# Convolution activations of a hybrid decoder layer mixed head by head and kept in DRAM

## The chip, the cores and the metric

The kernel runs on one core of one Trainium2 chip. The core has a matrix engine (TensorE, PE in the profile, with PEld for its weight loads), a vector engine (VectorE, DVE), a scalar engine (ScalarE, ACT), GpSimd (POOL) and SyncE (SP), which only issues transfers. Sixteen DMA engines move data between DRAM and the on-chip memory; here they are fed from two queues, SP's and POOL's. The metric is device time in microseconds of one execution, as the median of several runs. A profiled execution has a time of its own, which is given beside its span.

## The reference

One decoder layer on 528 tokens (16 learned meta tokens and a sequence of 512) of width 2048, in fp32:

```python
n = _rmsnorm(h, g_mix[l])
p = n @ w_in[l]
q, k, v, gb, gc, u = jnp.split(p, ...)            # six groups of 1024 columns
q = _rmsnorm(q.reshape(b, L, 8, 128), g_q[l]);  k = _rmsnorm(k.reshape(...), g_k[l])
o_attn = _stick_breaking_attention(q, k, v).reshape(b, L, 1024)
o_conv = gb * _causal_dwconv(gc * u, conv_w[l])   # 3 taps, one filter per channel
o = concat([_rmsnorm(o_attn, g_attn_out[l]), _rmsnorm(o_conv, g_conv_out[l])])
h = h + o @ w_out[l]
n2 = _rmsnorm(h, g_ffn[l])
h = h + (silu(n2 @ w_gate[l]) * (n2 @ w_up[l])) @ w_down[l]
```

The attention weights of a query t on a key s < t are beta[t,s] times the product of (1 - beta[t,j]) over the keys between them, computed in log space with a reverse cumulative sum. The meta positions are dropped from the output.

## The kernel before

All activations are held transposed: 128 channels on the partitions (a "k tile", 16 of them), tokens along the free dimension. To keep fp32 precision, each operand of a product is split into a high part (a cast to fp32r, on ACT) and a low part (the difference, on DVE), and each product is three matmuls: high x high, high x low, low x high. The helper split does this for activations, split_quad for weights.

The layer goes through these stages.

1. Start. SP loads the first weight pieces and the 16 tiles xt of x; ACT and DVE scale them by g_mix and split them into nh and nl (n_parts), which stay on chip. The products for k and q of head 0 run while this goes on (product_steps). Then read_qk evicts them.
2. Heads 0 to 7 (head). Each head's products for k, q and v run on PE over all 16 k tiles; the attention of the head (attend) is put between the matmuls of the next products: after(n, work) emits work n k tiles later, when tick has counted them. The masks of attend are made on POOL (causal). At the end of a head its output o is scaled and split into a tile st_o (a pool with two places) and stored to oa_dram on POOL's queue.
3. Convolution. The products for the first channel tile (pc0, pu0, pb0) and for pb1 run in the plain way. The other channel tiles go in pairs (conv_pair, gate_pair) by a scheme with seven block products in place of eight: pair_product. It takes two weight columns over two halves of the k tiles (four 512 KB weight blocks, "quads" 11, 12, 22, 21) and two halves of the tokens. Three weight operands are sums of quads (t1, t2, t3), and seven activation operands stand against the seven weights, in the order of conv_acts: a raw block of nh/nl, three mixed blocks (mixed), a last mixed block (last_block), and two more raw blocks.
4. The output projection, then the feed-forward in 44 pairs and the down projection by the same scheme. The change does not touch these.

The mixed blocks are differences of quarter blocks of x: with a0, a1 the two token halves of k tile k and b0, b1 those of k tile k + 8, they are d = b1 - a1, e = -d - a0, f = -e - b0, and for the last block a0 - a1. In the kernel before, mix_x (L706) is called for the eight k one after the other at L727, behind the work of the last head. For each k it loads the two rows of x again on POOL's queue, scales them on ACT, forms the four blocks on DVE, and splits three of them into the tiles mixed. The fourth is kept in late and is split at L737 over columns of nh and nl, which must not be read any more by the product pb1. pair_product for the first pair then starts with the product of the raw block 0 (x), goes on with the three mixed ones (z, x, z), the last block (x), the raw block 5 (y) and the raw block 6 (x).

What sets the order of the work: the program is written as one stream, and a scheduler orders each engine's instructions by its own estimate and by priorities; prepare marks weight splits as high priority, and tc.keep_in_program_order pins single instructions. Each engine and each queue runs its instructions in their order, and an instruction that waits holds up those behind it. Weights: next_w hands out split pieces and has two more prepared ahead; there are three places for split pieces, so a split waits until PE has finished the piece three before it. A loaded piece's place is loaded anew (load_wide, load_quad, load_next, on SP's queue) as soon as its split is done. For pairs in the "swapped" order (FIRST_ORDER, L223), the 21 quad is split first and used for the y product at the head of the pair; in the kernel before, that is the first feed-forward pair (i == CONV) alone.

Of the kernel before, what the change touches and what calls it, by code (L numbers as in the profile page):

```python
# [9 lines left out]
F32 = mybir.dt.float32  # L10
# [5 lines left out]
P = 128  # L16
# [17 lines left out]
def hybrid_layer(ctx: ExitStack, tc: tile.TileContext, xT, w_in, w_out, w_gu, w_down, vecs, out):  # L34
# [141 lines left out]
    def load_wide(g, i):  # L176

        if i < len(groups_w[g]):
            wide[g, i] = w_place(sw_in, 8, i % 4)
            nc.sync.dma_start(wide[g, i], groups_w[g][i])  # L180
        else:
            load_quad((0, CONV)[g], QUADS[i % 4])

    def load_next(i, q):

# [39 lines left out]
    def prepare():  # L225
        kind, i, s = pieces[len(split_w)]
        with tc.high_priority():
            if kind == "first":
                at = len(split_w)
                split_quad(raws[at], s - i, at % 6)  # L230
                if at % 2 and s % 8 == 0:
                    load_wide(0, s // 8 + 1)
                return
            if kind == "wide":
                split_quad(wide[i, s], 8)
                load_wide(i, s + 4)
                return
            n, swapped = pairs[i][0], i == CONV
            if swapped:
                s = FIRST_ORDER[s]  # L240
            b = {q: quads[i, q] for q in ("11", "12", "21", "22") if (i, q) in quads}
            if s == 0:
                split_quad(b["11"], n)
                add_quads(i, "t1", b["11"], b["12"])
                load_next(i, "11")
            elif s == 1:
                split_quad(sums["t1"], n)
                sums["t2"] = sums["t1"]
                ve.tensor_tensor(sums["t2"], sums["t2"], b["22"], ALU.add)
                if not swapped:  # L250
                    add_t3(i, b)
            elif s == 2:
                split_quad(sums["t2"], n)
                if swapped:
                    add_t3(i, b)
            elif s == 3:
                split_quad(b["22"], n)
                load_next(i, "22")
            elif s == 4:
                split_quad(sums["t3"], n)  # L260
            elif s == 5:
                split_quad(b["21"], n)
                if not swapped:
                    add_last(i, b)
            else:
                if swapped:
                    add_last(i, b)
                split_quad(sums["t2"], n)
                if i + 1 == SIX:
                    load_quad(SIX + 1, QUADS[1])  # L270

    def next_w():
        ahead = max(min(n_first, used[0] + 6), used[0] + 1 + S_AHEAD)
        while len(split_w) < min(len(pieces), ahead):
            prepare()
        used[0] += 1
        return split_w[used[0] - 1]
# [134 lines left out]
        for k in range(max(a, 1), b):  # L412
            load_x(k)
    for i in range(2):
        load_wide(0, i)
    for a, b in FIRST:
        for k in range(a, b):
            split_x(k)
# [13 lines left out]
    kns = [apool.tile([P, 640], F32, name=f"kn{i}") for i in range(1)]  # L432
    for t in kns:
        gp.memset(t[:, L:640], 0.0)
    accp.tile([P, 48], F32, name="pad_acc")
    acc_c = accp.tile([P, SEQ], F32, name="acc_c")
    acc_a = accp.tile([P, SEQ], F32, name="acc_a")

    stpool = open_pool("stpool")
    oa_dram = [dram.tile([P, 2, SEQ], F32R, name=f"oa_dram{h}") for h in range(HEADS)]  # L440

    def qk_norm(read, dst, parts_of, name):

# [25 lines left out]
    def head(h):  # L469

        if h:
            pk = pp.tile([P, 2, 512], F32, tag="pp", name=f"pk{h}")
            product([(pk[:, 0, :H], 0, H), (pk[:, 1, :H], H, L)], n_hl)
        read = read_qk(halves(pk, H), g_k, L) if h else read_k0
        kn = kns[0]
        kh = apool.tile([P, 384], F32R, tag="kh", name=f"kh{h}")
        kl = apool.tile([P, 384], F32R, tag="kl", name=f"kl{h}")
        after(8 if h else 19, qk_norm(read, kn[:, :L], (kh, kl, 384), f"k{h}"))

        if h:  # L480
            pq = pp.tile([P, 2, 512], F32, tag="pp", name=f"pq{h}")
            product([(pq[:, 0, :], META, L)], n_hl)
        read = read_qk(pq[:, 0, :], gq_s, SEQ) if h else read_q0
        qn = apool.tile([P, SEQ], F32, tag="qn", name=f"qn{h}")
        qh = apool.tile([P, SEQ], F32R, tag="qh", name=f"qh{h}")
        ql = apool.tile([P, SEQ], F32R, tag="ql", name=f"ql{h}")
        after(9 if h else 22, qk_norm(read, qn, (qh, ql, SEQ), f"q{h}"))

        pv = pp.tile([P, 2, 512], F32, tag="pp", name=f"pv{h}")
        product([(pv[:, 0, :H], 0, H), (pv[:, 1, :H], H, L)], n_hl)  # L490
        vt = t512(L, "e", 2)
        with tc.high_priority(0 if h else 1 << 20):
            ve.tensor_tensor(two(vt[:, :L]), halves(pv, H), two(r), ALU.mult)
        after(6 if h else 15, lambda: attend(h, kn, kh, kl, qn, qh, ql, vt))

    def attend(h, kn, kh, kl, qn, qh, ql, vt):
# [98 lines left out]
        def mix(ws):  # L595
# [7 lines left out]
            pe.matmul(o[:, Q0[3] :], v32[:, :P], lw[:, 1184:1328], start=False, stop=False)  # L603
            pe.matmul(o[:, Q0[4] :], v32[:16, P:], lw[:16, 1328:1344], start=False, stop=True)
            g = g_att[:, h : h + 1]
            st = stpool.tile([P, 2, SEQ], F32R, tag="st_o", bufs=2, name=f"st_o{h}")
            sc.activation(st[:, 0], o, AF.Copy, scale=g)
            ve.scalar_tensor_tensor(st[:, 1], o, g, st[:, 0].bitcast(F32), ALU.mult, ALU.subtract)
            square_sum(acc_a, o, h == 0)
# [21 lines left out]

    N = T2 + 2
    C0 = META - 2
# [11 lines left out]
    def gated(p, j, y, gb, s):  # L647
# [2 lines left out]
        square_sum(acc_c, p, j == 0, s, ve)  # L650
        sc.activation(p, p, AF.Copy, scale=g_cnv[:, j : j + 1])

    pc = cu_product("pc0")
    cu0 = t512(L, "e", 2)[:, : SEQ + 2]
    ve.tensor_tensor(cu0[:, :T2], pc[:, 0, :T2], r2[:, C0 : C0 + T2], ALU.mult)
# [9 lines left out]
    ve.tensor_tensor(gb0, pb[:, 0, :], r[:, META:], ALU.mult)  # L665
    assert not waiting
    apool.release()
    stpool.release()
    ocpool = open_pool("ocpool")

# [7 lines left out]
    const.release()  # L678

    mixp = open_pool("mixp")  # L680
    mixed = [mixp.tile([P, 8, 2, N], F32R, name=f"mixed{i}") for i in (1, 2, 3)]
    ctmp = open_pool("ctmp", side="right")

    def raw_block(kh, th, a=0, n=N):
# [1 line left out]
        return lambda part, k: n_parts[k + 8 * kh][part][:, at : at + n]  # L686

    def mixed_block(t, a=0, n=N):
        return lambda part, k: t[:, k, part, a : a + n]

    def last_block(a=0, n=N):
        return lambda part, k: n_parts[k][part][:, C0 + N + a : C0 + N + a + n]
# [8 lines left out]
        ]  # L701

    CN = SEQ + 2
    late = ctmp.tile([P, 8, N], F32, tag="late", name="late")

    def mix_x(k):  # L706

        x = []
        for i in range(2):
            if k % 2:  # L710
                x.append(ctmp.tile([P, 3 * N], F32, tag="sides", name=f"x{k}_{i}") if i else ctmp.tile([P, CN], F32, tag="b0", name=f"x{k}_{i}"))
                x[i] = x[i][:, :CN]
            else:
                x.append(ctmp.tile([P, CN], F32, tag="cu", bufs=2, name=f"x{k}_{i}"))
            gp.dma_start(x[i], xT[k + 8 * i][:, C0:])
            sc.activation(x[i], x[i], AF.Copy, scale=g_mix[:, k + 8 * i : k + 8 * i + 1])
        (a0, a1), (b0, b1) = ([t[:, i * T2 : i * T2 + N] for i in range(2)] for t in x)
        d, e = (oc_slot(1 + m, F32, f"mix{k}_{m}")[:, :N] for m in (k % 2, 2))
        ve.tensor_tensor(d, b1, a1, ALU.subtract)
        split(mixed[0][:, k, 0], mixed[0][:, k, 1], d)  # L720
        ve.scalar_tensor_tensor(e, d, -1.0, a0, ALU.mult, ALU.subtract)
        split(mixed[1][:, k, 0], mixed[1][:, k, 1], e)
        ve.scalar_tensor_tensor(d, e, -1.0, b0, ALU.mult, ALU.subtract)
        split(mixed[2][:, k, 0], mixed[2][:, k, 1], d)
        ve.tensor_tensor(late[:, k], a0, a1, ALU.subtract)

    for k in range(8):  # L727
        mix_x(k)
    gb1 = oc_slot(7, F32, "gb1")
    pb = pp.tile([P, 2, 512], F32, tag="pp", name="pb1")  # L730
    product([(pb[:, 0, :], META, L)], n_hl)
# [3 lines left out]
    xyz = open_pool("xyz", 2, space=PSUM)  # L735
    sm = open_pool("sm2", 1, space=PSUM)
    for k in range(8):  # L737
        split(*(n_parts[k][part][:, C0 + N : C0 + 2 * N] for part in range(2)), late[:, k])
    sides_c = ctmp.tile([P, 3 * N], F32, tag="sides", name="sides_c").rearrange("p (a b) -> p a b", a=3)

    def wide_product(ps, acts):
        hi, lo = next_w()
# [27 lines left out]
    def pair_product(acts, cols, out2, side, fourth=None):  # L770
# [30 lines left out]
    def conv_pair(j):  # L801
        u = ctmp.tile([P, CN], F32, tag="cu", bufs=2, name=f"cu{j}")
        y, last = pair_product(conv_acts(), N, [u[:, t * T2 : t * T2 + N] for t in range(2)], [sides_c[:, t] for t in range(3)])
        ve.tensor_tensor(u, u, r2[:, C0:], ALU.mult)
        c = sides_c[:, 0, :T2]
        ve.tensor_tensor(c, y[:, :T2], c, ALU.add)
        ve.tensor_tensor(u[:, :T2], u[:, :T2], c, ALU.mult)
        x = last()
        ve.tensor_tensor(u[:, T2:], x, u[:, T2:], ALU.mult)
        ocf[j] = ctmp.tile([P, 8 * N], F32, tag="late", name="y6")[:, :SEQ] if j == 6 else oc_slot(min(j, 6), F32, f"y{j}")  # L810
        conv3(ocf[j], u, j)

    def gate_pair(j):
# [10 lines left out]
        gated(ocf[j - 1], j - 1, ocf[j - 1], b0, b0)  # L824

    def scale_a():
        w = ctmp.tile([P, 8 * N], F32, tag="late", name="work_a")
        w = [w[:, i * SEQ : (i + 1) * SEQ] for i in range(3)]
# [377 lines left out]
```

## Time and profile before

| | |
|---|---|
| median of 3 runs | 2065.96 us (2065.57 to 2066.32) |
| the profiled execution | 2066.83 us, its span 2065.1 us |
| mean granted clock of TensorE | 0.993 |
| DMA | 339.35 MB, mean 164 GB/s |
| POOL's queue | 77616 packets, 124.33 MB |

A row of waits names the engine and the tile that it was about to write, then what it waited for, then the time in total, the number of waits and the longest. A row of a timeline gives the start and the duration in microseconds, the engine and line, the operation, the tiles written and read, shapes and types, and in brackets the idle time of the engine before it. A row of stages gives the stretch, its length, the busy time of PE, PEld, DVE, ACT and POOL with the number of instructions, the granted clock, the busy share of the DMA engines and the rate. Matmul rows overlap: the distance between the starts of two is their pace. In a group, a tile's number is left out, so pb is pb0 and pb1.

### The profile page before, as it was taken

To read this page: it belongs to the slowest core of one execution; us is meant where nothing else is said; L and a number is where in the kernel's file an instruction comes from. 1 tells how busy PE (TensorE), PEld (TensorE's weight loads), DVE (VectorE), ACT (ScalarE), POOL (GpSimd) and SP (SyncE) were. 2 spreads that over 40 slices of the span, in tenths; PEclk is the share of its full clock that TensorE was granted. 3 is DMA by queue.
4 is the path that set the end of the run, shared out by engine and by line. 5 is a ranking of instruction groups with operands and counts; after the bars stand their busy time and mean duration, and the time that the engine had idled before them with its cause. 6 is when DMAs were issued, how large, how long until landed. Compare 5 with 4: busy or idle time off the path is not lost.

```text
span 2065.1 us, 39541 instructions
## 1 busy us (share of the span) xinstructions
PE 2034.2 (99%) x16134; PEld 1968.8 (95%) x16134; DVE 1744.4 (84%) x2243; ACT 1071.1 (52%) x1551; POOL 347.0 (17%) x501
## 2 busy tenths in 40 slices
PE   9999999889999999999999999999999999999999
PEld 8999999789998888999999999999999999999999
DVE  6877777788888778999898898898888888888888
ACT  6666556544444444555455555555555544444443
POOL 0111111200003442111111111011011243121111
PEclk9999999989999999999999999999999999999999
DMA  6222222433345555546545555465555899798764
GB/s 213 76 92 83 93 93 82 140 96 103 103 161 192 168 171 191 164 139 194 169 139 174 159 154 169 149 173 159 147 175 158 255 335 348 191 297 209 218 148 94
DMA packets 145254, 339.35 MB, mean 164 GB/s; under 512 B 12768, under 2 KB 60640, under 8 KB 145072
## 3 DMA queue, kind: packets, MB, share of 16 engines
q1 hardware_dynamic: 67456, 212.50, 32.1%
q0 software_dynamic: 77616, 124.33, 22.9%
q8 instruction: 126, 2.06, 0.4%
q14 instruction: 56, 0.46, 0.1%
HBM read 267.31 MB, written 69.47 MB: 163 GB/s over the span
## 4 chain that ended last, share of the span: by engine, by line
PE 91%; DVE 3%; DMA 3%; ACT 1%; issue 1%; SPq 0%; POOL 0%; DVEq 0%; ACTq 0%; POOLq 0%
PE x L766 13%; PE x L768 13%; PE x L767 13%; PE z L767 6%; PE z L766 6%; PE z L768 6%; PE y L767 3%; PE y L766 3%; PE y L768 3%; PE pv L302 2%; PE pv L303 2%; PE pv L304 2%; PE pq L303 1%; PE pq L304 1%; PE pq L302 1%; PE pk L302 1%
## 5 line engine op out<-in xcount | busy, mean ns | idle before, releaser
L202 ACT CAST sw_split<-sw_in 128x1024 fp32r<-128x1024 f32 (+2 forms) x668 | 661.9, 992 | 708.8 <-PE z L767 190.8
L203 DVE TENSOR_TENSOR sw_split<-sw_in,sw_split 128x1024 fp32r<-128x1024 f32 (+2 forms) x668 | 771.6, 1156 | 165.2 <-ACT sw_split L202 156.8
L766 PE MATMUL x<-f,sw_split 128*128 128x256 f32 x1408 | 387.6, 275 | 0.1
L768 PE MATMUL x<-f,sw_split 128*128 128x256 f32 x1408 | 387.4, 275 | 0.1
L767 PE MATMUL x<-f,sw_split 128*128 128x256 f32 x1408 | 387.3, 275 | 0.0
L766 PEld LDWEIGHTS x<-f,sw_split 128*128 128x128 f32 x1408 | 264.3, 188 | 0.4 <-ACT sides L790 0.3
L768 PEld LDWEIGHTS x<-f,sw_split 128*128 128x128 f32 x1408 | 264.3, 188 | 0.3 <-DVE sw_split L203 0.3
L767 PEld LDWEIGHTS x<-f,sw_split 128*128 128x128 f32 x1408 | 264.3, 188 | 0.1
L1021 POOL DMA_DIRECT2D fd<-s x147 | 103.8, 915 | 711.5 <-DVE s L316 694.8
L209 DVE TENSOR_TENSOR sw_in<-sw_in 128x1024 f32<-128x1024 f32 (+1 forms) x164 | 187.9, 1146 | 10.4 <-DMA sw_in<-w_gu 3.2
L767 PE MATMUL z<-f,sw_split 128*128 128x256 f32 x704 | 193.7, 275 | 1.4 <-DVE f L316 1.4
L766 PE MATMUL z<-f,sw_split 128*128 128x256 f32 x704 | 193.7, 275 | 1.0 <-ACT sides L788 1.0
L768 PE MATMUL z<-f,sw_split 128*128 128x256 f32 x704 | 193.6, 275 | 0.0
L768 PE MATMUL x<-ring,sw_split 128*128 128x256 f32 x608 | 167.3, 275 | 0.5 <-DVE sw_split L203 0.5
L766 PE MATMUL x<-ring,sw_split 128*128 128x256 f32 x608 | 167.2, 275 | 0.0
L767 PE MATMUL x<-ring,sw_split 128*128 128x256 f32 x608 | 167.2, 275 | 0.0
L767 PEld LDWEIGHTS z<-f,sw_split 128*128 128x128 f32 x704 | 132.1, 188 | 1.6 <-DVE f L316 1.6
L766 PEld LDWEIGHTS z<-f,sw_split 128*128 128x128 f32 x704 | 132.1, 188 | 1.2 <-ACT sides L788 1.2
L768 PEld LDWEIGHTS z<-f,sw_split 128*128 128x128 f32 x704 | 132.1, 188 | 0.0
L768 PEld LDWEIGHTS x<-ring,sw_split 128*128 128x128 f32 x608 | 114.1, 188 | 0.7 <-DVE sw_split L203 0.7
L766 PEld LDWEIGHTS x<-ring,sw_split 128*128 128x128 f32 x608 | 114.1, 188 | 0.0
L767 PEld LDWEIGHTS x<-ring,sw_split 128*128 128x128 f32 x608 | 114.1, 188 | 0.0
(609 smaller groups left out, 5486.2 us busy)
## 6 DMA issues: line engine op xcount, KB each, us to landing
sw_in<-w_gu SPq DMA_DIRECT2D x176, 512.0 KB, 4.0
sw_in<-w_in SPq DMA_DIRECT2D x92, 512.0 KB, 3.3
fd<-s POOLq DMA_DIRECT2D x147, 256.0 KB, 5.3
sw_in<-w_down SPq DMA_DIRECT2D x96, 384.0 KB, 4.3
ring<-fd POOLq DMA_DIRECT2D x42, 768.0 KB, 16.7
sw_in<-w_out SPq DMA_DIRECT2D x32, 512.0 KB, 3.5
out_T<-d POOLq DMA_DIRECT2D x54, 256.0 KB, 5.0
sw_in<-w_down SPq DMA_DIRECT2D x16, 512.0 KB, 7.5
```

The source lines that it names most:

```text
L202: sc.copy(hi, src)
L203: ve.tensor_tensor(lo, src, hi.bitcast(F32), ALU.subtract)
L209: return ve.tensor_tensor(sums[name], a, b, ALU.add)
L302: pe.matmul(ps, wh, ah[:, a:b], start=k + i == 0, stop=False)
L303: pe.matmul(ps, wh, al[:, a:b], start=False, stop=False)
L304: pe.matmul(ps, wl, ah[:, a:b], start=False, stop=k + i == last)
L766: pe.matmul(p, hi[:, kk], ah, start=start and j == k == 0, stop=False, skip_group_check=skip)
L767: pe.matmul(p, hi[:, kk], al, start=False, stop=False, skip_group_check=skip)
L768: pe.matmul(p, lo[:, kk], ah, start=False, stop=k == n - 1, skip_group_check=skip)
L1021: gp.dma_start(fd[c][s][:, :, k], t[:, :, i])
```

## The change

The mixed blocks are no longer made behind the last head. Head h from 1 to 7 makes k tile h - 1, and the eighth is made beside pc0. Each k tile is loaded as four pieces of 128x258 (load_mix, on POOL's queue), scaled by two ACT instructions of 516 columns, mixed in place by four DVE instructions of 258, split two blocks at a time into a place of the pool of st_o (stage), and stored as four pieces of 128x516 to DRAM tensors mix_dram, again on POOL's queue. Behind the last head, six loads on POOL's queue bring the three mixed blocks into tiles mixed (two halves each), and sixteen loads bring the last block into the columns of nh and nl. late and its splits are gone.

The first convolution pair takes the swapped order as well: its y product, on a raw block, comes first, and its 21 quad is split first. Two small parts stand beside this: the first two wide weight loads are pinned to program order, and next_w prepares one piece less ahead at the one call where the first pieces run out. Tiles that stood for the first use of a tag in apool are declared ahead, so that places come out the same.

```diff
@@ load_wide / prepare / next_w
-            nc.sync.dma_start(wide[g, i], groups_w[g][i])
-        else:
-            load_quad((0, CONV)[g], QUADS[i % 4])
+            return nc.sync.dma_start(wide[g, i], groups_w[g][i])
+        load_quad((0, CONV)[g], QUADS[i % 4])
...
-            n, swapped = pairs[i][0], i == CONV
+            n, swapped = pairs[i][0], i in (0, CONV)
...
-        ahead = max(min(n_first, used[0] + 6), used[0] + 1 + S_AHEAD)
+        ahead = max(min(n_first, used[0] + 6), used[0] + 1 + S_AHEAD - (used[0] == n_first))
...
-        load_wide(0, i)
+        tc.keep_in_program_order(load_wide(0, i))
@@ new, ahead of the heads
+    mix_dram = [dram.tile([P, 8, 2, N], F32R, name=f"mix_dram{i}") for i in range(4)]
+    xpool2 = open_pool("xpool2")
...
+    def stage(name):
+        return stpool.tile([P, 4 * N], F32R, tag="st_o", bufs=2, name=name)
+
+    def load_mix(k):
+        x = xpool2.tile([P, 4, N], F32, tag="x", name=f"x_mix{k}")
+        for m in range(4):
+            at = C0 + m % 2 * T2
+            gp.dma_start(x[:, m], xT[k + m // 2 * 8][:, at : at + N])
+        return x
+
+    def mix_x(k, x):
+        for i in range(2):
+            sc.activation(x[:, 2 * i : 2 * i + 2], x[:, 2 * i : 2 * i + 2], AF.Copy, scale=g_mix[:, k + 8 * i : k + 8 * i + 1])
+        a0, a1, b0, b1 = (x[:, m] for m in range(4))
+        ve.tensor_tensor(b1, b1, a1, ALU.subtract)
+        ve.tensor_tensor(a1, a0, a1, ALU.subtract)
+        ve.scalar_tensor_tensor(a0, b1, -1.0, a0, ALU.mult, ALU.subtract)
+        ve.scalar_tensor_tensor(b0, a0, -1.0, b0, ALU.mult, ALU.subtract)
+        for m, blocks in ((2, (2, 0)), (0, (1, 3))):
+            st = stage(f"st_x{k}_{m}").rearrange("p (a b n) -> p a b n", a=2, b=2)
+            split(st[:, :, 0], st[:, :, 1], x[:, m : m + 2])
+            for i, block in enumerate(blocks):
+                gp.dma_start(mix_dram[block][:, k], st[:, i])
@@ head
+            x = load_mix(h - 1)
             pq = pp.tile([P, 2, 512], F32, tag="pp", name=f"pq{h}")
...
+        if h:
+            after(5, lambda: mix_x(h - 1, x))
@@ attend
-            st = stpool.tile([P, 2, SEQ], F32R, tag="st_o", bufs=2, name=f"st_o{h}")
+            st = stage(f"st_o{h}")[:, : 2 * SEQ].rearrange("p (a b) -> p a b", a=2)
@@ convolution
+    x = load_mix(7)
+    after(3, lambda: mix_x(7, x))
     pc = cu_product("pc0")
...
-    mixed = [mixp.tile([P, 8, 2, N], F32R, name=f"mixed{i}") for i in (1, 2, 3)]
+    mixed = [[mixp.tile([P, 4, 2, N], F32R, name=f"mixed{i}_{m}") for m in range(2)] for i in (1, 2, 3)]
+    for i, t in enumerate(mixed):
+        for m in range(2):
+            gp.dma_start(t[m], mix_dram[i][:, 4 * m : 4 * m + 4])
...
-    late = ctmp.tile([P, 8, N], F32, tag="late", name="late")
-    def mix_x(k):
...
-    for k in range(8):
-        mix_x(k)
...
     for k in range(8):
-        split(*(n_parts[k][part][:, C0 + N : C0 + 2 * N] for part in range(2)), late[:, k])
+        for part in range(2):
+            gp.dma_start(n_parts[k][part][:, C0 + N : C0 + 2 * N], mix_dram[3][:, k, part])
...
-        first = i == CONV
+        first = i in (0, CONV)
```

More of the change, by code (lines that the diff above doesn't have):

```diff
@@ L434, in hybrid_layer @@
         gp.memset(t[:, L:640], 0.0)
+    for tag, n in (("kh", 384), ("kl", 384), ("sh", L), ("sl", L), ("qn", SEQ), ("qh", SEQ), ("ql", SEQ), ("bh", 288), ("bl", 288)):
+        apool.tile([P, n], F32 if tag == "qn" else F32R, tag=tag, name=f"first_{tag}")
     accp.tile([P, 48], F32, name="pad_acc")
@@ L439, in hybrid_layer @@
     stpool = open_pool("stpool")
+    N = T2 + 2
+    C0 = META - 2
+    mix_dram = [dram.tile([P, 8, 2, N], F32R, name=f"mix_dram{i}") for i in range(4)]
+    xpool2 = open_pool("xpool2")
     oa_dram = [dram.tile([P, 2, SEQ], F32R, name=f"oa_dram{h}") for h in range(HEADS)]
+    def stage(name):
[19 more added lines that the diff above has]
+                gp.dma_start(mix_dram[block][:, k], st[:, i])
     def qk_norm(read, dst, parts_of, name):
@@ L630, in token_scale @@
         rsqrt(dst, v, SEQ, y, t, eng)
-    N = T2 + 2
-    C0 = META - 2
     def cu_product(name):
@@ L667, in hybrid_layer @@
     apool.release()
+    xpool2.release()
     stpool.release()
@@ L688, in mixed_block @@
     def mixed_block(t, a=0, n=N):
-        return lambda part, k: t[:, k, part, a : a + n]
+        return lambda part, k: t[k // 4][:, k % 4, part, a : a + n]
     def last_block(a=0, n=N):
@@ L703, in hybrid_layer @@
     CN = SEQ + 2
-    late = ctmp.tile([P, 8, N], F32, tag="late", name="late")
-    def mix_x(k):
[L708 to L725, printed above, removed]
-    for k in range(8):
-        mix_x(k)
     gb1 = oc_slot(7, F32, "gb1")
@@ L737, in hybrid_layer @@
     for k in range(8):
-        split(*(n_parts[k][part][:, C0 + N : C0 + 2 * N] for part in range(2)), late[:, k])
-    sides_c = ctmp.tile([P, 3 * N], F32, tag="sides", name="sides_c").rearrange("p (a b) -> p a b", a=3)
+        for part in range(2):
+            gp.dma_start(n_parts[k][part][:, C0 + N : C0 + 2 * N], mix_dram[3][:, k, part])
+    sides_c = ctmp.tile([P, 3, N], F32, name="sides_c")
     def wide_product(ps, acts):
@@ L809, in conv_pair @@
         ve.tensor_tensor(u[:, T2:], x, u[:, T2:], ALU.mult)
-        ocf[j] = ctmp.tile([P, 8 * N], F32, tag="late", name="y6")[:, :SEQ] if j == 6 else oc_slot(min(j, 6), F32, f"y{j}")
+        ocf[j] = ctmp.tile([P, SEQ], F32, tag="work0", name="y6") if j == 6 else oc_slot(min(j, 6), F32, f"y{j}")
         conv3(ocf[j], u, j)
@@ L826, in scale_a @@
     def scale_a():
-        w = ctmp.tile([P, 8 * N], F32, tag="late", name="work_a")
-        w = [w[:, i * SEQ : (i + 1) * SEQ] for i in range(3)]
+        w = [ctmp.tile([P, SEQ], F32, tag=f"work{i}", name=f"work_a{i}") for i in range(3)]
         token_scale(acc_a, acc_a, 1024, "a", (oc_slot(6, F32R, "acc_hi"), oc_slot(7, F32R, "acc_lo"), *w))
```

## The prediction

> **What bounds the kernel now.** I read the page's busy times and chain first, then the waits of TensorE (PE), then the stages around the longest wait, then PE's instructions there.
>
> ```profile
> PE 2034.2 (99%) x16134; PEld 1968.8 (95%) x16134; DVE 1744.4 (84%) x2243; ACT 1071.1 (52%) x1551; POOL 347.0 (17%) x501
> PE 91%; DVE 3%; DMA 3%; ACT 1%; issue 1%; SPq 0%; POOL 0%; DVEq 0%; ACTq 0%; POOLq 0%
> ```
>
> PE sets the end: a microsecond in which it stands still, or runs at half clock, is a microsecond of the kernel. Its longest waits:
>
> ```profile
> PE z L766 <- ACT mixed L315: 10.2, 3, 5.1
> PE z L766 <- DVE gb L732: 5.6, 1, 5.6
> PE pv L302 <- ACT tmp L397: 2.3, 1, 2.3
> ```
>
> The first two lie at one place, the first convolution pair, where the mixed blocks are made while PE waits for them. The stages there (PE, PEld, DVE, ACT, POOL busy; granted clock; DMA share; GB/s):
>
> ```profile
> 100.00:380.00 280.00, 280.00 (x1911) 261.82 (x1910) 207.84 (x342) 168.56 (x277) 39.30 (x103) 1.00 0.27 88
> ...
> 396.00:400.00 4.00, 3.11 (x25) 2.89 (x23) 4.00 (x9) 2.45 (x5) 1.16 (x3) 1.00 0.67 192
> 400.00:404.00 4.00, 0.00 (x0) 0.00 (x0) 3.25 (x10) 2.93 (x8) 1.08 (x2) 0.97 0.30 81
> 404.00:412.00 8.00, 4.67 (x15) 3.58 (x15) 7.28 (x20) 6.15 (x14) 2.69 (x5) 0.50 0.49 138
> 412.00:420.00 8.00, 2.32 (x6) 1.50 (x6) 6.93 (x19) 5.58 (x14) 1.07 (x2) 0.50 0.62 189
> 420.00:424.00 4.00, 1.26 (x3) 0.79 (x3) 2.64 (x8) 2.78 (x6) 0.00 (x0) 0.50 0.00 0
> ...
> 428.00:432.00 4.00, 4.00 (x35) 4.00 (x35) 1.22 (x1) 1.45 (x3) 0.00 (x0) 1.00 0.00 0
> ```
>
> In the heads (100 to 380) PE has no gap. From 399 to 428 it is nearly empty, at clock 0.50, while VectorE (DVE) is the busiest. PE's own rows give the size:
>
> ```profile
> 395.78 0.39 PE L625 MATMUL ss_a<-acc_hi,ones_r 128*128 128x512 f32 x1
> 396.01 0.28 PE L766 MATMUL x<-nh,sw_split 128*128 128x258 f32 x1
> ...
> 428.93 0.28 PE L766 MATMUL z<-mixed,sw_split 128*128 128x258 f32 x1
> ...
> 431.79 0.28 PE L766 MATMUL x<-nh,sw_split 128*128 128x258 f32 x1
> ```
>
> One product of 24 matmuls takes 431.79 - 428.93 = 2.86 us unhindered. The pair's first product starts at 396.01, its fifth at 431.79; unhindered that would be 396.01 + 4 x 2.86 = 407.45. The place costs **24.3 us**, half clock included.
>
> **The change, part by part.**
>
> *Taken from the pair.* The 8 calls of mix_x and the 8 late splits leave this place, and with them their waits. The same seven products remain, so the gain is at most 24.3. Putting the y product first leaves the sum of products alone; it moves the first use of a mixed block from 396.01 + 2.86 = 398.9 to 396.01 + 2 x 2.86 = 401.7. Its weights are the "21" quad, the last of the four to be loaded:
>
> ```profile
> 378.36 1.22 DVE L203 TENSOR_TENSOR sw_split<-sw_in,sw_split 128x1024 fp32r<-128x1024 f32 x1
> 384.65 1.05 ACT L202 CAST sw_split<-sw_in 128x1024 fp32r<-128x1024 f32 x1 [1.34 <-PE pb L303]
> ```
>
> The first row is the split of the last wide piece; the quad's load takes that piece's place from 379.6 on and has 5 us until its own split, which takes the turn of the second row. So y can start at 396, and nothing is added.
>
> *Put in its place: loads on POOL's queue.* In the built program the queue holds five 0.13 MB loads into nh/nl, the six mixed loads (128x2064 f32, 1.06 MB each), then eleven more small ones. The fifth waits until PE has read nh2 in pb1: pb1 is 48 matmuls ending at 395.78, at 0.23 each it starts at 384.6, so at 386.7; the mixed loads queue behind that. Behind them POOL has nothing until the row at 608. What a load of this kind takes (two-microsecond stages, the issue, the landing of single ones):
>
> ```profile
> 608.14 2.13 POOL L843 DMA_DIRECT2D oa<-oa_dram  x4 [190.42 <-DVE sw_split L203]
> ...
> 612.00:614.00 2.00, 2.00 (x19) 2.00 (x18) 1.27 (x2) 0.57 (x1) 1.32 (x3) 1.00 1.12 408
> ...
> 620.00:622.00 2.00, 2.00 (x19) 1.96 (x19) 2.00 (x4) 1.37 (x3) 0.00 (x0) 1.00 1.15 426
> 946.00:949.00 3.00, 3.00 (x29) 3.00 (x28) 2.03 (x3) 1.05 (x1) 1.34 (x3) 1.00 0.98 235
> L715 POOL DMA_DIRECT2D x<-xT x16: 537/537/562, 384.8 to 417.2; - x16
> DMA to landing us min/median/max: 2.9/3.1/4.2
> ```
>
> From 612 to 622 the attention output is loaded beside weights, 4 KB per partition: 408 to 426 GB/s. At 946 a load stands behind stores of 1 KB rows: 235. Up to the last mixed half, 0.66 + 6.34 MB plus about three weight quads (1.57) move, 8.57 MB. At 410 that is 20.9 us: 386.5 + 20.9 = 407.4, about 408 landed. It is needed in the middle of the fifth product, 407.45 + 1.4 = 408.9. The last four small loads wait for mixed halves by their semaphores: 408 + 4 x 0.54 + 3.1 = 413.3, needed at 410.3 + 7/8 x 2.86 = 412.8. So the wait is about 0.5, with no margin. Ends: 0, and at 235 GB/s 8.57/0.235 = 36.5 us, 423, a wait of 14. I take **+1.5**, nearer to the 410 row because these rows are 8 KB long.
> [...]
>
> *Added to the heads.* Per head and for head 0 of the start, in durations of the old rows:
>
> ```profile
> L716 ACT ACTIVATE x<-x,vec 128x514 f32<-128x514 f32 x16 | 11.2, 724 | 5.3 <-DMA x<-xT 5.3
> L316 DVE TENSOR_TENSOR mixed<-mix,mixed 128x258 fp32r<-128x258 f32 x24 | 9.6, 422 | 0.6 <-ACT mixed L315 0.5
> 258.11 0.56 POOL L610 DMA_DIRECT2D oa_dram<-st_o  x1 [9.70 <-DVE st_o L608]
> 260.60 0.62 ACT L315 CAST qh<-qn 128x512 fp32r<-128x512 f32 x1 [2.15 <-DVE qn L461]
> 261.25 0.69 DVE L316 TENSOR_TENSOR ql<-qn,qh 128x512 fp32r<-128x512 f32 x1
> 265.12 0.39 PE L516 MATMUL z<-ql,kh 128*128 128x512 f32 x1
> 271.43 0.69 POOL L533 TENSOR_SCALAR_AFFINE_SELECT sp<-sp 128x128 f32<-128x128 f32 x3 [11.42 <-DVE sp L545]
> 285.46 0.67 DVE L316 TENSOR_TENSOR spl<-lw,sph 1x512 fp32r<-1x512 f32 x1
> 287.11 0.40 PE L576 MATMUL c<-spl,carry 128*128 128x512 f32 x1
> 303.14 0.69 DVE L316 TENSOR_TENSOR ql<-qn,qh 128x512 fp32r<-128x512 f32 x1
> oa_dram<-st_o POOLq DMA_DIRECT2D x8, 512.0 KB, 3.0
> ```
>
> DVE: 4 x 0.42 + 2 x 0.69 = 3.1 us; ScalarE (ACT): 2 x 0.72 + 2 casts x 0.62 = 2.7; POOL: 8 DMA issues x 0.54 = 4.3. A head is 303.14 - 261.25 = 41.9 us, so DVE goes from 207.84/280 = 74% to 82%, ACT from 60% to 67%. The cover is PE's margin: ql is ready at 261.94 and read at 265.12; in the new order a weight split (1.15) and the split of st_x (0.6) stand ahead of it, 1.4 us remain. spl is ready at 286.13 and read at 287.11: 1.0 us; ahead of it on DVE now stands one 0.34 us step, and two of 0.6 have moved behind it. POOL's stores wait for DVE and its masks stand behind them, but POOL idles 11.42 us there. ACT's two scalings of x stand ahead of the casts sph; they need x_mix, whose loads stand behind the stores (estimate: issued by 267.5, landed by 271.5) and so come about when ACT is free, near 271. Below, a gain is excluded: PE has no gap there. Above, all of ACT's 2.7 us on the path of 7 heads: 19. I take **+1.0** in all, because the margins quoted all stay positive. The two st_o places now serve three uses per head: st_o, then both halves of st_x. The second half takes st_o's place, whose store is issued at 258.1 and lands 3.0 later, 261.1; its cast on ACT comes about 261.8 (260.60 plus the 1.2 that now stands ahead of qh), so it costs nothing by 0.7 us; late, it would hold up the cast of vh behind it.
>
> *Added to the start.* The first x_mix load (0.53 MB) is issued about 3 us in, its stores (1.06 MB) and the next load (0.53) when DVE has split it, among the last nl steps: an estimate of 26 to 31.
>
> ```profile
> 8.00:24.00 16.00, 15.45 (x92) 12.47 (x92) 14.09 (x25) 12.86 (x22) 0.00 (x0) 1.00 0.92 327
> ...
> 28.00:30.00 2.00, 2.00 (x16) 1.92 (x15) 0.00 (x0) 0.38 (x1) 0.00 (x0) 1.00 0.93 375
> 30.00:32.00 2.00, 1.38 (x6) 0.77 (x5) 1.30 (x2) 2.00 (x3) 0.00 (x0) 1.00 0.04 14
> ...
> 34.00:40.00 6.00, 6.00 (x39) 6.00 (x39) 4.91 (x9) 5.78 (x11) 0.00 (x0) 0.72 0.63 212
> 33.71 0.39 PE L302 MATMUL pv<-nh,sw_split 128*128 128x264 f32 x1 [2.33 <-ACT tmp L397]
> ```
>
> Until 24 the DMA is nearly full, so 0.53/0.327 = 1.6 us if nothing is spare; near 28 the three weight loads that the splits ahead of L397 need share with the stores: up to 1.59/0.375 = 4.2. The end above is 5.8, the one below 0 (two queues together reach 410 against 327 here); added bytes bring nothing forward. I take 1.0 + 1.5 = **+2.5**. [...]
>
> *First weight splits, SP order.* In the built program the three splits ahead of L397 stand in the same order and places as before, and SP's loads too: 0. A change of ties there could move 1 us either way.
>
> *Sum* against the profiled 2066.83 (span 2065.1): -24.3 + 1.5 + 1.0 + 2.5 = -19.3, 2047.5. The median shown is 0.87 below that run, so **2046.6**.
>
> **The rivals.**
> 1. *The wait goes over to the DMA* (PE z on mixed landing): 235 to 300 GB/s gives waits of 6 to 14 in place of 1.5, 2051 to 2059, say 2055. For it: 16 small loads of 1 KB rows and weights in the same stretch. Against: the 408 and 426 rows.
> 2. *The heads' chain lengthens*: 1.3 us in each of 7 heads, +9 in place of 1, 2055. For: margins of 1.0 and 1.4. Against: 26% of DVE idle.
> 3. *The start pays its upper end*, 5.8 in place of 2.5: 2050.
> 4. *Slower than before*: POOL's stores hold up the masks in every head, for a DVE split or for DMA places; place: between the o store and L533. The 8 issues on the path cost 4.3 x 7 = 30 in place of 1: 2076. It decides from (24.3 - 4.0)/7 = 2.9 us per head. Against: POOL's 11.42 us.
> 5. *The change does not do it*: the blocks become usable as late as now, since the loads wait on POOL for what PE still has to read. Only y's 2.86 us would be covered, against 3.5 of bills: 2066.6. Against: the loads wait for nothing later than nh2 at 386.7.
>
> **Chances.** Forecast 65% (from 2066.83 - 24.3 - 0.87 = 2041.7, with every bill 0, to 2050); rival 1 13%; 2 10%; 3 6%; 4 4%; 5 2%. Range 2041 to 2057: it leaves out 4, 5 and the worst of 1. 0.2% (4.1 us) is about what a measurement can tell from no change. Faster 0.94, within 0.2% 0.02, slower 0.04.
>
> **What would show it.** Right: the wait on "ACT mixed" gone, PE full from 396 on but for up to 2 us on a DMA of mixed or nh/nl, clock 1.00 there, pv's first matmul 2 to 3 us later than 33.71, heads at 42 us. Wrong: windows between 400 and 420 with PE under 9 of 10, heads over 43 us, or pv past 38.

## The result, and the profile after

The changed kernel takes 2051.65 us (median of 4 runs, 2049.61 to 2053.62) beside 2066.14 us before; the ratio is 0.9926, 95% interval 0.9908 to 0.9943. That is 14.5 us, inside the forecast range of 2041 to 2057, but 5 us above the forecast of 2046.6. The profiled execution took 2049.99 us, its span 2048.3.

From the page of the changed kernel, busy times and chain:

```profile
PE 2031.4 (99%) x16134; PEld 1966.7 (96%) x16134; DVE 1743.4 (85%) x2227; ACT 1066.5 (52%) x1535; POOL 382.8 (19%) x571
PE 89%; DMA 4%; DVE 3%; issue 1%; ACT 1%; POOL 1%; SPq 0%; DVEq 0%; ACTq 0%; POOLq 0%
```

Its longest waits of PE (total, times, longest):

```profile
PE z L779 <- DVE f L315: 1.9, 1, 1.9
PE pv L301 <- ACT tmp L396: 1.6, 1, 1.6
PE ss_q L484 <- ACT sh_q L314: 1.4, 1, 1.4
...
PE x L779 <- DMA nl<-mix_dram: 1.1, 1, 1.1
```

And its stages (PE, PEld, DVE, ACT, POOL busy; granted clock; DMA share; GB/s):

```profile
100.00:380.00 280.00, 278.06 (x1889) 259.81 (x1889) 223.17 (x377) 180.29 (x301) 65.68 (x153) 0.99 0.39 124
...
388.00:392.00 4.00, 4.00 (x19) 3.24 (x18) 1.90 (x3) 2.18 (x4) 3.89 (x8) 1.00 0.70 156
...
396.00:400.00 4.00, 4.00 (x25) 3.52 (x24) 1.37 (x2) 1.05 (x1) 0.92 (x2) 1.00 1.05 420
400.00:404.00 4.00, 4.00 (x35) 4.00 (x34) 2.79 (x3) 1.05 (x1) 0.67 (x2) 1.00 1.08 428
404.00:412.00 8.00, 8.00 (x67) 7.86 (x66) 5.78 (x7) 3.97 (x6) 1.06 (x2) 1.00 1.07 407
412.00:420.00 8.00, 6.77 (x45) 5.69 (x44) 3.62 (x5) 1.16 (x2) 2.11 (x4) 1.00 1.07 303
420.00:424.00 4.00, 4.00 (x34) 3.88 (x33) 3.96 (x6) 1.10 (x2) 0.00 (x0) 1.00 0.06 20
```

The hole between 399 and 428 is closed: PE is full at clock 1.00 but for 1.2 us behind 412, and the DMA does in that place what DVE did before. The gaps are not all that is lost there: from 412 to 420 PE starts 45 matmuls, in the 8 us before it 67, so more is lost than the gaps show. The heads are new: 278.06 of 280 us, where before PE had no gap.

PE's instructions at the borders of the stages and at the waits, first of the changed kernel, then the three of the kernel before that the prediction doesn't show:

```profile
33.88 0.39 PE L301 MATMUL pv<-nh,sw_split 128*128 128x264 f32 x1 [1.62 <-ACT tmp L396]
...
84.69 0.40 PE L484 MATMUL ss_q<-sh_q,ones_r 128*128 128x512 f32 x1
...
126.72 0.49 PE L484 MATMUL ss_q<-sh_q,ones_r 128*128 128x512 f32 x1 [1.42 <-ACT sh_q L314]
127.74 0.56 PE L485 MATMUL ss_q<-sl_q,ones_r 128*128 128x512 f32 x1 [0.53 <-DVE sl_q L315]
...
398.28 0.39 PE L658 MATMUL ss_a<-acc_hi,ones_r 128*128 128x512 f32 x1
...
419.42 0.39 PE L779 MATMUL x<-nl,sw_split 128*128 128x258 f32 x1 [1.07 <-DMA nl<-mix_dram]
...
442.46 0.29 PE L778 MATMUL x<-nh,sw_split 128*128 128x258 f32 x1
...
794.96 0.39 PE L779 MATMUL z<-f,sw_split 128*128 128x256 f32 x1 [1.85 <-DVE f L315]
797.03 0.79 PE L661 MATMUL ss_h<-work_r,ones_r 128*128 128x512 f32 x1 [1.00 <-DVE work_r L315]
```

```profile
86.04 0.40 PE L454 MATMUL ss_q<-sh_q,ones_r 128*128 128x512 f32 x1
...
461.09 0.29 PE L766 MATMUL x<-nh,sw_split 128*128 128x258 f32 x1
...
815.58 0.50 PE L628 MATMUL ss_h<-work_r,ones_r 128*128 128x512 f32 x1 [0.97 <-DVE work_r L316]
```

Differences of these starts make the account of the two profiled executions. The row at 442 (461 before) is the first matmul of the third pair, so the row above it holds the first two pairs.

| stage | before | after | change |
|---|---|---|---|
| start, to pv of head 0 | 33.71 | 33.88 | +0.2 |
| to ss_q of head 1 | 52.33 | 50.81 | -1.5 |
| to ss_a behind pb1 | 309.74 | 313.59 | +3.9 |
| first two pairs | 65.31 | 44.18 | -21.1 |
| third pair to ss_h | 354.49 | 354.57 | +0.1 |
| ss_h to the end of the span | 1249.5 | 1251.3 | +1.7 |

The sum is -16.8, as the spans have it. The -1.5 and the +1.7 are one stretch of half clock each, which the changed kernel did not have behind the start (its clock is 1.00 up to 128.03; before, it was 0.50 from 35.09 to 38.50) and did have at 797 (0.50 from 797.05 to 800.46). A third, 0.50 from 128.03 to 131.44, is inside the +3.9.

### The profile page after: what moved, and what is told of

Read it like the earlier page. It is cut to its first block, busy times and chain, and to the rows that moved or that the text cites. A ratio compares the mean times of both kernels' runs of the same rounds, so it can differ in the third digit from the quotient of the medians.

```text
span 2048.3 us, 39668 instructions
## 1 busy us (share of the span) xinstructions
PE 2031.4 (99%) x16134; PEld 1966.7 (96%) x16134; DVE 1743.4 (85%) x2227; ACT 1066.5 (52%) x1535; POOL 382.8 (19%) x571
## 4 chain that ended last, share of the span: by engine, by line
PE 89%; DMA 4%; DVE 3%; issue 1%; ACT 1%; POOL 1%; SPq 0%; DVEq 0%; ACTq 0%; POOLq 0%
PE x L778 13%; PE x L779 13%; PE x L780 13%; PE z L778 6%; PE z L779 6%; PE z L780 6%; PE y L778 3%; PE y L780 3%; PE y L779 3%; PE pv L301 1%; PE pv L302 1%; PE pv L303 1%; DMA sw_in<-w_down 1%; PE pq L303 1%; PE pq L301 1%
```

## The experiments

All were compared with the kernel before on their chip. PE has the same matmuls in each. The rows stand in three groups of four, each on one chip, where the kernel before took 2065.93, 2067.16 and 2067.14 us; between groups, medians are up to 1.2 us apart for that alone, and the ratios are what can be compared.

| run | median, us | ratio to before, 95% interval |
|---|---|---|
| as_changed | 2050.80 | 0.9925 (0.9913 to 0.9937) |
| store_earlier | 2047.90 | 0.9912 (0.9898 to 0.9926) |
| small_on_sp | 2052.43 | 0.9934 (0.9920 to 0.9947) |
| both | 2048.26 | 0.9916 (0.9903 to 0.9930) |
| y_not_first | 2049.69 | 0.9911 (0.9898 to 0.9925) |
| heads_only | 2071.01 | 1.0017 (1.0008 to 1.0026) |
| late_start | 2051.34 | 0.9919 (0.9905 to 0.9932) |
| kept_order | 2045.67 | 0.9890 (0.9875 to 0.9905) |
| no_small | 2047.15 | 0.9902 (0.9886 to 0.9917) |
| order_alone | 2065.77 | 0.9992 (0.9983 to 1.0001) |
| store_earlier_again | 2046.91 | 0.9905 (0.9891 to 0.9918) |
| kept_order_again | 2045.83 | 0.9899 (0.9885 to 0.9912) |

The two small edits (the pinned wide loads, one piece less ahead) were not run by themselves, so what they are worth is not shown.

**The changed kernel again.**

> The changed kernel again, as the measure for the three beside it. In its profile PE stands still 1.4 + 0.5 us at the q norm of head 2 (126.72 and 127.74) and runs 3.4 us at half clock behind it; 1.1 us at the last block (419.42); 1.9 us at 794.96 with 3.4 us at half clock behind it. Theory: a gap of 1.4 to 2 us is sometimes followed by half clock, sometimes not, each such stretch costs 1.7 us, so runs lie in steps of about 1.7 between some 2048 and 2054. Rival: the time differs for another reason, then the mean granted clock doesn't go with the time.

Its five runs lie between 2046.84 and 2053.24. The profiled one is the fastest, and its granted clock is 1.000; of the four runs above, that at 2049.61 has 0.999, that at 2049.99 has 0.998, and those at 2053.31 and 2053.62 have 0.997. So time and clock go together, as the theory has it, but not to the end: the other four runs here all have 0.998 and lie between 2049.85 and 2053.24, 3.4 us apart, while 0.001 of the mean clock stands for 2 us. Some of the spread has another cause, which stays open (the start alone varies by 1.9 us between profiles, see below). How the clock falls is shown by stretches of 3.41 us, the length of each half clock in the changed kernel (from 128.03 and from 797.05) and of the first in the kernel before (from 35.09; the second, from 403.73, lasts 23.89, seven times that). First the changed kernel, then its second profile, then the run late_start:

```profile
32.46:35.87 3.41, 1.99 (x16) 2.00 (x17) 2.68 (x3) 3.41 (x8) 0.46 (x2) 1.00 1.04 305
124.62:128.03 3.41, 1.47 (x8) 0.95 (x7) 3.41 (x6) 2.68 (x6) 0.15 (x1) 1.00 0.43 136
128.03:131.44 3.41, 3.41 (x15) 3.25 (x15) 3.10 (x5) 1.57 (x2) 0.14 (x1) 0.50 0.06 20
793.64:797.05 3.41, 1.10 (x7) 0.86 (x7) 3.41 (x6) 1.05 (x1) 0.00 (x0) 1.00 0.21 85
797.05:800.46 3.41, 3.41 (x15) 3.32 (x16) 2.96 (x5) 1.26 (x2) 0.00 (x0) 0.50 0.02 5
```

```profile
790.98:794.39 3.41, 1.69 (x14) 1.44 (x12) 2.50 (x4) 0.81 (x2) 0.00 (x0) 1.00 0.56 226
794.39:797.80 3.41, 2.43 (x20) 2.18 (x19) 3.41 (x6) 1.51 (x3) 0.00 (x0) 1.00 0.02 5
```

```profile
794.71:798.12 3.41, 1.78 (x11) 1.50 (x12) 3.41 (x8) 1.05 (x1) 0.00 (x0) 1.00 0.06 25
798.12:801.53 3.41, 3.41 (x19) 3.41 (x18) 2.34 (x3) 1.26 (x2) 0.00 (x0) 0.50 0.22 61
```

A stretch in which PE worked 1.10 or 1.47 of 3.41 us is followed by one at 0.50, as is one of 1.38 in the kernel before (31.68 to 35.09); after 1.69 and 1.99 it is not, but after the 1.78 of late_start it is. Each stretch at 0.50 costs 1.7 us (3.41 x 0.50). The two gaps at 794 stand in one stretch for 2.31 us in the first profile (3.41 - 1.10), and in two stretches, with 1.72 and 0.98 us, in the second.

**The late load in the heads.**

```diff
-            split(st[:, :, 0], st[:, :, 1], x[:, m : m + 2])
-            for i, block in enumerate(blocks):
-                gp.dma_start(mix_dram[block][:, k], st[:, i])
+            with tc.high_priority(400 if k == 1 and m == 0 else 0):
+...
```

> Only the second split of the mixed tile in head 2 (k = 1), its two stores and with them the next x_mix load stand earlier in the queues: two masks of POOL go behind them. Theory L (the load of x_mix is late and ScalarE, which runs in order, stands 4.7 us on it ahead of sh_q): the gaps of 1.4 and 0.5 us at the q norm go, and the half clock behind them; 2046.5 for a run of which the rest is as profiled (2050.0 - 1.9 - 1.7). Rival W (ScalarE's added work itself, 2 x 0.72 and 2 x 0.62 us, makes sh_q late): the gap stays above 1 us, 2050.

In the changed kernel's timeline, POOL, DVE and ACT beside head 1's attention and head 2's products (POOL's masks stand between its first two rows):

```profile
97.04 1.07 POOL L470 DMA_DIRECT2D mix_dram<-st_x  x2
...
111.74 0.68 DVE L315 TENSOR_TENSOR st_x<-x_mix,st_x 128x516 fp32r<-128x516 f32 x1
...
113.39 1.08 POOL L470 DMA_DIRECT2D mix_dram<-st_x  x2
114.46 2.17 POOL L454 DMA_DIRECT2D x_mix<-xT  x4
...
121.55 0.73 ACT L460 ACTIVATE x_mix<-x_mix,vec 128x516 f32<-128x516 f32 x1 [4.73 <-DMA x_mix<-xT]
...
126.06 0.61 ACT L314 CAST sh_q<-tmp 128x512 fp32r<-128x512 f32 x1
```

and with the second split and its stores ahead:

```profile
105.02 1.05 POOL L470 DMA_DIRECT2D mix_dram<-st_x  x2 [5.20 <-DVE st_x L315]
...
107.17 0.56 POOL L454 DMA_DIRECT2D x_mix<-xT  x1
...
123.47 0.62 ACT L314 CAST sh_q<-tmp 128x512 fp32r<-128x512 f32 x1
```

The scheduler had put the second half of the tile (subtraction on DVE, two stores, and behind them the next x_mix load) 16 us after the first, where it is 5.5 us in the next heads. Most of that is DVE's order: the subtraction ran at 111.74, and the mask ahead of the stores held them only 1.0 us more. The load then landed at 121.5; ACT, in order, stood 4.73 us on it, and sh_q came late. With the load 9.0 us earlier (counted from head 1's ss_q, at 84.69 and 86.35) that wait and both gaps at ss_q are gone; from head 1's ss_q to ss_a it takes 309.89 us (before 309.74). So seven heads' mixing costs 0.2 us, and one misplaced load cost 3.9 with the half clock behind it; the second profile of the changed kernel drew none there (clock 1.00 from 125.38 to 132.20), and takes 311.70, 2.0 more than before. Theory L holds; the runs, 2046.4 to 2048.7, also lie closer together.

**Where the last block's loads go.**

```diff
-            gp.dma_start(n_parts[k][part][:, C0 + N : C0 + 2 * N], mix_dram[3][:, k, part])
+            nc.sync.dma_start(n_parts[k][part].bitcast(F32)[:, C0 + N : C0 + 2 * N], mix_dram[3].bitcast(F32)[:, k, part])
```

> The 16 small loads of the last block go on SP's queue (read as f32, the same bytes), so POOL issues the six mixed loads right behind the last o store, 2.6 us earlier (388.1 in place of 390.8). Theory Q (POOL's queue is what is late: the small loads wait there for mixed halves to land, L750 <- DMA mixed, 14.5 us in all): the waits of the sixth product, 1.07 and some 1.3 in pieces, go, -2.4, so 2047.6 for a run of which the rest is as profiled. Rival R (the rate: 400 to 428 GB/s from 396 to 412 is all there is): only the earlier start counts, and the weights behind the small loads on SP's queue come late instead; the time stays within 1 us of 2050, and PE waits for a split instead.

Theory Q missed. Waits of PE, then of DVE, in that run:

```profile
PE x L780 <- DVE sw_split L202: 4.2, 2, 3.7
...
DVE sw_in L208 <- DMA sw_in<-w_in: 5.1, 2, 3.3
```

The small loads now hold up the weights behind them on SP's queue, where they wait 14.5 us for others of them to land and 4.7 for PE: PE stands 3.7 us on a weight split, half clock follows (0.65 in the mean from 420 to 424), and the first two pairs take 47.5 us in place of 44.2. That is rival R's wait on a split, though the median is 1.6 us above as_changed and not within 1. A queue change moved the wait to another queue.

> Both edits. If theories L and Q hold, -3.6 and -2.4 add up: about 2044 for a run of which the rest is as profiled, and the runs lie closer together, as two gaps that half clock could follow are gone. If only L holds 2046.5, if only Q 2047.6, if none 2050.

2048.26 us: the head's gain is there (ss_a 360.63 us behind pv), and so is the loss in the pairs (47.54). Only L held; but it came out 1.8 us above the 2046.5 of that case, as Q did not end at nothing.

**How much the small loads cost.** The 16 loads are left out; the last block reads a raw half instead.

> The changed kernel without the 16 small loads: the last block's product reads the raw second token half of the same tiles in place of a0 - a1, so the output is another one; PE has the same matmuls. In the profile of the changed kernel the first two pairs take 44.1 us from the last matmul ahead of them, of which 2 x 20.3 + 0.4 = 41.0 is work; 3.1 is lost. Theory S (the small loads lose it: 2.7 us of issue ahead of the mixed ones, then their own late landing): the loss falls below 0.7, 2048.3 beside 2050.8. Rival M (mixed loads and weights at some 420 GB/s lose it): more than 2 of the 3.1 stay, 2050 to 2051.

PE's two border rows, and two stages:

```profile
400.94 0.39 PE L658 MATMUL ss_a<-acc_hi,ones_r 128*128 128x512 f32 x1
...
442.45 0.29 PE L778 MATMUL x<-nh,sw_split 128*128 128x258 f32 x1
```

```profile
408.00:416.00 8.00, 8.00 (x69) 8.00 (x68) 5.77 (x7) 3.38 (x7) 0.00 (x0) 1.00 0.50 144
416.00:420.00 4.00, 4.00 (x33) 3.88 (x33) 3.40 (x6) 1.88 (x2) 0.00 (x0) 1.00 0.47 148
```

442.45 - 400.94 = 41.5 us for the two pairs: of the 3.1 lost, 2.6 went with the small loads, and PE has no gap there. Theory S holds; the 6.3 MB of mixed blocks are in time beside the weights. The median's fall (3.7, on another chip) is more than the pairs show; what makes up the rest is not shown, the chance of the clock among the candidates.

**All mixed loads first.** On top of store_earlier:

```diff
-            gp.dma_start(t[m], mix_dram[i][:, 4 * m : 4 * m + 4])
+            tc.keep_in_program_order(gp.dma_start(t[m], mix_dram[i][:, 4 * m : 4 * m + 4]))
...
-            gp.dma_start(n_parts[k][part][:, C0 + N : C0 + 2 * N], mix_dram[3][:, k, part])
+            tc.keep_in_program_order(gp.dma_start(n_parts[k][part][:, C0 + N : C0 + 2 * N], mix_dram[3][:, k, part]))
```

> The kernel of store_earlier, with the mixed loads and the small loads pinned to program order: all six mixed loads go ahead of all sixteen small ones, on POOL's queue as before, so no small load waits for pb1 ahead of them; they are issued from some 388.1 in place of 390.8, into a stretch where the DMA moved 156 GB/s. Theory E (2.6 us of earlier start carry through to the end of the loads): the waits of the sixth product, 1.2 us and some 1.3 in pieces, go: 2045.5 beside 2047.9. Rival (the small loads behind, one at a time as places of the queue come free, end as late as before): 2047.9 within 0.7 us.

The queue in the changed kernel, for comparison, and below it the queue, PE's borders and its wait on a weight split with the pinned order:

```profile
388.11 0.57 POOL L750 DMA_DIRECT2D nl<-mix_dram  x1 [0.75 <-PE pb L303]
...
390.76 3.21 POOL L717 DMA_DIRECT2D mixed<-mix_dram  x6
...
412.17 0.53 POOL L750 DMA_DIRECT2D nh<-mix_dram  x1 [2.72 <-DMA mixed<-mix_dram]
...
415.58 0.54 POOL L750 DMA_DIRECT2D nl<-mix_dram  x1
```

```profile
384.36 3.23 POOL L717 DMA_DIRECT2D mixed<-mix_dram  x6
...
395.34 0.39 PE L658 MATMUL ss_a<-acc_hi,ones_r 128*128 128x512 f32 x1
...
410.31 0.53 POOL L750 DMA_DIRECT2D nl<-mix_dram  x1 [1.03 <-DMA nl<-mix_dram]
...
438.75 0.29 PE L778 MATMUL x<-nh,sw_split 128*128 128x258 f32 x1
...
PE x L780 <- DVE sw_split L202: 1.4, 2, 0.9
```

Measured from ss_a, the mixed loads start 3.5 us earlier (11.0 ahead of it in place of 7.5) and the last small one goes out 2.3 earlier (15.0 behind it in place of 17.3). No wait on a load is left, but the pairs fell only from 44.1 to 43.4: a wait of 0.9 us on a weight split came in its place. The medians, of two chips, fell by 2.2; both were run once more side by side.

> The kernel of store_earlier, so that kept_order can be compared with it on one chip. By the traces the pinned order is worth 0.7 us in the pairs (44.10 to 43.40); the medians of two separate comparisons differ by 2.2. Theory G (half clock, which follows a gap or not by chance, made up the rest): the two medians now differ by 0.5 to 1.5. Rival: by 2 or more.

> The kernel of kept_order beside store_earlier_again: 0.5 to 1.5 us below it by theory G, 2 or more by its rival.

2046.91 and 2045.83, 1.1 apart, where theory G has them; the pairs take 44.48 and 43.34 us. The runs of the two overlap (2046.32 to 2048.44 and 2044.17 to 2047.66), and that the clock made up the rest is not shown. The pinned order is the fastest of the kernels, some 5 us below the changed one and 21 below the one before.

**The order of the pair.** The changed kernel with the first pair in the old order:

> The changed kernel with the first pair in its old order: the raw block 0 first, then the mixed blocks, the y product behind the last block. Everything that is loaded is now needed 2.86 us earlier. Theory D (the loads set the end of the pair: the last mixed half was put to use as it landed, near 411.9): PE waits 2 to 3 us more on mixed halves and small loads, with a chance of half clock behind it, so 2053 to 2055.5 beside 2050.8. Rival (the loads have slack, the order is worth nothing): 2050.8 within 1 us.

```profile
PE z L778 <- DMA mixed<-mix_dram: 1.8, 2, 1.5
```

The waits move to the mixed halves, as theory D says, but the two pairs take 45.0 us in place of 44.1, and the ratio, 0.9911, is not above the changed kernel's 0.9925. D's 2 to 3 us missed: most of what PE waited for early it did not wait for at the end.

> The kernel before, with the y product first in the first pair and nothing else. Theory P (PE waits for blocks that DVE makes; y is 2.86 us of work that can be done while it waits, and its weights cost DVE the same two steps, earlier): 0 to 2.9 us faster, 2063.5 to 2066. Rival (the early weights stand ahead of the blocks on DVE, 2.4 us): nothing gained or up to 2 slower, 2066 to 2068.

Without the stored blocks the order shows no more: the pairs take 65.17 in place of 65.31 us, and the interval, 0.9983 to 1.0001, holds 1. The median is 1.4 us below that of the kernel before on this chip, which theory P allows, but with 0.1 us in the pairs the two theories are not told apart.

**The bill without the gain.**

> The mixing in the heads with its loads and stores as in the changed kernel, but nothing is read back: the first pair makes its blocks itself, in the old order, as before. It shows the bill without the gain. Theory H (one late load in head 2 and little else): pv's first matmul up to 1 us later, gaps of 1.2 to 1.9 us in head 2, sometimes half clock behind them: 2067 to 2070 beside 2066. Rival (all seven heads pay, 1.3 us each or more): 2075 and above. Rival (the bill is nothing): 2066.

1.0017 (1.0008 to 1.0026) and medians 3.9 us apart. In its profile pv starts at 34.56, and ss_a comes 364.34 us later, 2.3 more than before. Up to head 1's ss_q that is 50.78, near the 50.81 of the changed kernel, which had no half clock there, in place of 52.33 before, with the half clock from 35.09 to 38.50; from head 1's ss_q on it is 313.56 us, 3.8 more, at a granted clock of 0.99 from 100 to 380 (1.00 before). The gaps in head 2 are the same 1.4 and 0.5. That is theory H's mechanism, at the upper end of its price (1 to 4 us above the kernel before).

> The changed kernel with the first x_mix tile held back until the k product of head 1 is evicted: its load, its mixing and its stores leave the start and go into head 1. Theory A (at the start x_mix costs up to 1 us, in a start that varies by as much from run to run): pv's first matmul near 33.7, 2049.8 to 2051. Rival B (the start paid the forecast 2.5 us): 2048.3. Rival C (the work of the start was free and is now in the way of head 1): a gap in head 1, 2052 or more.

```profile
92.78 0.50 PE L634 MATMUL o<-wh,vh 128*128 128x512 f32 x1 [1.16 <-ACT wh L314]
```

pv starts at 34.02. The three profiles without x_mix at the start (before, order_alone, late_start) have pv at 33.7 to 34.1, mean 33.9; the eleven with it at 33.8 to 35.7, mean 34.6. The start's bill is 0.7 us, with a spread of 1.9 between the eleven; theory B's 2.5 is out. But the median, 2051.34, lies between theory A's range and rival C's, and the trace speaks for C's mechanism: there is a gap of 1.2 us in head 1 and two of 0.5 and 0.6 at 140.65 and 163.46, in place of those at ss_q, and from head 1's ss_q to ss_a it takes 313.92 us, 2.2 more than as_changed, with no half clock in it: the run's mean clock, 0.999, leaves room for the stretch at 798 alone (1.7 of 2048.4 us; two would make it 0.998). The heads lost more than the start gained.

## Why the prediction was right and wrong

**The gain, 24.3: right.** The two pairs fell from 65.3 to 41.5 us where nothing was left to wait for, 23.8; the work in them is some 2 x 20.3 + 0.4 = 41.0.

**Mixed loads late, +1.5: 3.1.** The step that failed is "The last four small loads wait for mixed halves by their semaphores", which put them at 413.3. The mixed halves themselves came nearly as forecast: pb1 ended 2.5 us later than before, and the last half landed and was read at 411.7, 409.2 on the old clock, against 408 landed and 408.9 needed. But of the small loads behind the mixed ones eight of the last nine, from 396.69 on, waited for the landing of the load eight places ahead of them in the queue (six times a mixed half, 14.5 us of POOL standing still), so they went out one by one, and PE's wait ended at 419.42 where 415.8 was forecast (413.3 + 2.5). The five small ones ahead of the mixed loads cost too: 2.7 us of issue, with the DMA at 156 GB/s from 388 to 392. The rate forecast, 410 GB/s, was 407 to 428 from 396 to 412. That the rate was not what cost it is shown by no_small too: PE has no gap there at 421 to 425 GB/s from 396 to 408.

**Heads, +1.0: 0.2 in the work, 3.9 in all.** The margins of the quoted head held in each head that has this order. The step that failed is to cost seven heads by one: beside head 1's attention the built program has the second subtraction, its stores and the x_mix load late, behind the masks, and this could be read from the order of the program ahead of any run. It is rival 4's place (POOL's queue between the o store and the masks) with the roles turned round: the masks did not wait for the stores; the stores and the load behind them came late, in one head. Of the 3.9, 1.7 is half clock that this execution drew behind the gaps. "Heads over 43 us" was named as the sign; one head longer by 4 us is what came.

**Start, +2.5: 0.7** in the mean of the profiles, 0.2 in this execution, which had no half clock behind it (1.00 up to 128.03). The upper half of the range came from counting bytes as if the startup had no slack. That the sum of start and heads, 3.5, was met by heads_only, 3.9, is luck: the start cost less and one head more.

**Half clock: left out.** The sum took the one such stretch at the start of the kernel before (0.50 from 35.09 to 38.50, behind a gap of 2.33 us) as given and none elsewhere. In the two profiles of the changed kernel it differs: the first drew two stretches, at 128 and at 797, together 3.4 us, the second none (mean clock 1.000); the gap ahead of the one at 797 is there before the change too (1.38, and 1.0 to 1.8 in the experiments). Nor is it always one stretch: at 793 in kept_order, behind gaps of 1.81 and 1.00 us, matmuls start 0.21 us apart in place of 0.11 from 793.86 to 799.20, longer than 3.41. By terms, with the start of this execution (+0.2, and -1.5 for the half clock it did not have): -24.3 + 3.1 + 3.9 + 0.2 - 1.5 + 1.7 = -16.9, against -16.8 in the traces. Beside the forecast's -19.3 the mixed loads cost 1.6 more, the heads 2.9 more and the half clock at 797 another 1.7, while the start came 3.8 cheaper, 1.5 of it by the draw of the clock. So the profiled execution is only 2.5 us from the forecast in part because errors cancelled. The five us between forecast and median are these 2.5, the 1.7 by which the median lies above the profiled execution, and the 0.9 that the forecast took off for the median before.

**The rivals.** Rival 1's place was right and its sign small: 1.1 us on a small load, not on a mixed one. Rivals 2 and 4 are out, as one head paid and not seven; so is rival 3, as pv came at most 2.0 us later in eleven profiles. Rival 5 is out: the mixed blocks were in time, though with nothing to spare, since PE waits 1.8 us for them when y is not first.

## What to carry to other kernels

Work that is spread over repetitions is to be costed in each of them by the built order, not in one by its margins: in POOL's queue, which goes in order, one store that the scheduler put 16 us late made here a late load (landed at 121.5), an idle ScalarE (4.73 us) and a stall of PE (1.42 and 0.53 us). The small loads behind large ones on one queue went out one by one here as earlier ones landed (eight of the last nine waited, six of them 14.5 us); put the large ones first, and count the small ones' issue and landing as the end of the chain. Gaps of 1.85 and 1.00 us at one place of the changed kernel cost 1.7 us more in one profile, and 1.72 and 0.98 us nothing more in another. So a profile shows one draw: compare stages in the traces before medians.

## What the runs showed of the hardware

Half clock lasted 3.41 us from 128.03 and from 797.05 in the changed kernel and from 35.09 in the kernel before, and 23.89 us, seven times that, from 403.73 there. Laid out in stretches of this length from those points, the two profiles have from 5.2 us on four with less than 1.99 us of PE's work at full clock, and these are the four ahead of the falls (1.47, 1.10, 1.38 and 0.00 us). In other runs one with 1.69 us (as_changed) was not followed by half clock, and one with 1.78 us (late_start) was. In the changed kernel the DMA kept 407 to 428 GB/s from 396 to 412, with the 8 KB rows of the mixed blocks and 4 KB rows of weights, and moved 303 GB/s at the same busy share (1.07) from 412 to 420, with 1 KB rows of the last block beside weights (1.27 and 1.15 MB).
